# Output projection and MLP: squares in their own tiles, x of two residuals and the first MLP operands loaded ahead, sums of later quarters started earlier

## The chip, the cores and the metric

The kernel runs on one core of a Trainium2 chip. TensorE (PE) multiplies, VectorE (DVE) and ScalarE (ACT) do elementwise work, GpSimd (POOL) does little here, and SyncE (SP) issues nearly all transfers. The metric is the device time of one execution in microseconds (us).

## The reference

One layer of a hybrid decoder over 2048 tokens of width 1024, all in float32. Two token mixers fill `mix`; then come the output projection, the MLP and a gated embedding:

```python
mix_out = jnp.einsum('btc,cd->btd', mix, w_out[i])
h = h + rms_norm(mix_out, post_mix_norm[i])

u = jnp.einsum('btd,df->btf', rms_norm(h, pre_mlp_norm[i]), w_mlp_up[i])
y = jnp.einsum('btf,fd->btd', jnp.square(jax.nn.relu(u)), w_mlp_down[i])
h = h + rms_norm(y, post_mlp_norm[i])

e = rms_norm(jnp.einsum('bte,ed->btd', p[i], w_ple_proj[i]), ple_norm[i])
gate = jax.nn.sigmoid(jnp.einsum('btd,de->bte', h, w_ple_gate[i]))
h = h + e * gate
```

`rms_norm(x, w)` is x · rsqrt(mean(x²) + eps) · w over the width. The MLP is 4096 wide.

## The kernel before

Each float32 operand is split into a high part (a copy by ACT to fp32r, line 165 or 218) and a low part (a subtraction by DVE, line 166 or 219), and a product of 128x128 by 128x512 is three matmuls: high·high, high·low, low·high. Work is transposed: a tile holds 128 of the width and a quarter of 512 tokens.

**Output projection (about 1122 to 1307 us).** The loop over `order` takes quarter q = 0..3 and block d = 0..7; each pair is 24 matmuls `mmo`, and ACT copies the bank to `yo` (line 1361). For q = 0 and 1 ACT also squares the bank into `sq_o` and DVE adds it to `acc_o` (lines 228, 229). `sq` is one tile, shared by `sq_o`, `sq_h` and `rr`. At the end of quarters 0 and 1 `normed` starts: `rstd_steps` sums over the width by two matmuls with ones (`nrm_o`, lines 1152 and 1153, from `hl_o`, the split of `acc_o`), then makes the reciprocal root (Ln, Exp, one correction step); `residual` scales each of the eight blocks, adds x (loaded two at a time into `late` tiles, `xo`), stores h to `h1d`, and sums the squares in `acc_h`; a second `rstd_steps` (`nrm_h`) gives the scale for the MLP. For q = 2 and 3 `yo` goes to memory (`yod`) and its norm comes later.

`w_out` is split anew for quarters 0 to 2. For the last quarter, blocks below `RESTS` load the raw weights and the stored low part, and ACT makes the high part (line 349); the others are loaded split from a 1 MB cache (line 186).

**MLP up, half 0 (from about 1307 us).** Sixteen groups g, each seven Strassen products of 12 matmuls (`u`, 84 matmuls a group). The moving operands `t11 .. t22` come from `early_operands` (`be`, quarter 0) and `up_operands` (`b`, quarter 1), which load h from `h1d` and scale it; `run(prep)` finishes what is left of them before the MLP. The weights of the next group (`a`, `s`, split as `wu`) are prepared by `up_weights` between the products. DVE adds each product into `u` (line 1471) and forms `ht` (1452 to 1455). `summed(q)` squares quarters 2 and 3 from `yod` (`nrm_o2`, `nrm_o3`), and `passed(q)` makes their residual (`yp`, `xp`, `nrm_h2`, `nrm_h3`).

**What sets the order.** Every eight matmuls a tick runs an agenda. `later(gen, steps)` gives a generator's next step to the tick with that offset. PE's order is the order of the code with its ticks; in the output projection the orders of DVE, ACT and SP are set by a scheduler. On each engine the queue then runs in order, so an instruction that waits holds all behind it. Moving operands lie in 28 ring slots, `y` in 16 tiles, `stg` in two.

Of the kernel before, what the change touches and what calls it, by code (L numbers as in the profile page):

```python
# [10 lines left out]
F32 = mybir.dt.float32  # L11
# [4 lines left out]
ALU = mybir.AluOpType  # L16
# [68 lines left out]
def trunk(ctx, tc, x, xT, pT, vecs, w_in, w_ab, gdn_a_log, gdn_dt_bias, w_out, w_up, w_down,  # L85
# [38 lines left out]
    def col(r):  # L124
        return cols[:, r : r + 1]
# [95 lines left out]
    def squares(acc, src, k, name, eng=V):  # L221

        if acc is None:
            acc = st.tile([P, QT], F32, tag="acc", name=f"acc_{name}", bufs=3)
            S.activation(acc, src, AF.Square)
        else:
            sq = st.tile([P, QT], F32, tag="sq", name=f"sq_{name}_{k}", bufs=1)
            S.activation(sq, src, AF.Square)  # L228
            eng.tensor_tensor(acc, acc, sq, ALU.add)  # L229
        return acc  # L230
# [905 lines left out]
    def ytile(name):  # L1136
        return f2.tile([P, QT], F32, tag="y", name=name, bufs=16)
# [38 lines left out]

    kept_rows = []

    def residual(q, y_of, rsb, skip, gain, dst, name, sums=None):

        xk = late(skip(0), f"x{name}{q}_0")
        y = y_of(0)
        total, put = None, None
        for d in range(KD):
            yield
            if put:
                nc.sync.dma_start(*put)
            if d + 1 < KD:
                nxt, ynxt = late(skip(d + 1), f"x{name}{q}_{d + 1}"), y_of(d + 1)
            V.scalar_tensor_tensor(y, y, col(gain + d), rsb, ALU.mult, ALU.mult)  # L1190
            V.tensor_tensor(y, y, xk, ALU.add)
# [8 lines left out]
    def normed(q, ys, acc, skip, gain, dst, name, sums=None, pool=None):  # L1200

        rd = []
        yield from rstd_steps(acc, 1.0 / D, EPS, f"{name}{q}", rd.append, pool)
        total = yield from residual(q, lambda d: ys[d], rd[0], skip, gain, dst, name, sums)
# [38 lines left out]
    def moving(half, n, k, raw):  # L1243
        x = next_pool().tile([P, 2, QT], F32R, tag="ring", name=f"t{n}_{half}_{k}")
        split(x, V, raw)
        tops[half][n].append(x)

    def start_operands(half):
        tops[half] = {n: [] for n in ("11", "3", "1", "2", "21", "4", "22")}

    first_b = {}

    def early_operands():

        start_operands(0)
        for k in range(KD // 2):
            for n, kk in (("11", k), ("21", k + KD // 2)):
                b = first_b[kk] = ytile(f"be_{kk}")
                nc.sync.dma_start(b, h1d[0][kk])
                V.scalar_tensor_tensor(b, b, col(R_PREMLP + kk), h1_r[0], ALU.mult, ALU.mult)  # L1260
                moving(0, n, k, b)
                yield

    def up_operands(half, rsb):

        qs = (2 * half, 2 * half + 1)
        early = half in tops
        if not early:
            start_operands(half)
        for k in range(KD // 2):  # L1270
            n = f"{half}_{k}"
            b11, b21, b12, b22, t3, t2, t4 = (once(lambda i=i: ytile(f"b{i}_{n}")) for i in range(7))
            if early:
                b11, b21 = (lambda k=k: first_b[k]), (lambda k=k: first_b[k + KD // 2])
            for b, s, kk in ((b12, 1, k), (b22, 1, k + KD // 2), (b11, 0, k), (b21, 0, k + KD // 2)):
                if early and s == 0:
                    continue
                nc.sync.dma_start(b(), h1d[qs[s]][kk])
                V.scalar_tensor_tensor(b(), b(), col(R_PREMLP + kk), rsb[s], ALU.mult, ALU.mult)
# [45 lines left out]
    for j, (q, d) in enumerate(order):  # L1325
        if d == 0:
            ys, acc = [], None
            if q < 2:
                later(mix_operands(q + 1), range(2, 18, 2))
            if q == 1:  # L1330
                later(mix_operands(3), range(17, 25))
        ready_out(j + 2)
        stage_out(j + 3)
        if j == len(order) - 5:
            u_raw = [wp.tile([P, 2, QT], F32, tag="raw", name=f"u_raw{i}", bufs=2) for i in range(2)]
            a1, a2 = w_up[0], w_up[FF // P // 2]
            for t, i, src in ((u_raw[0], 0, a1[:, : KD // 2]), (u_raw[1], 1, a1[:, KD // 2 :]),
                              (u_raw[0], 1, a2[:, : KD // 2]), (u_raw[1], 0, a2[:, KD // 2 :])):
                nc.sync.dma_start(t[:, i].rearrange("p (k n) -> p k n", n=P), src)
        if j == len(order) - 2:  # L1340
            two_blocks(("11", u_raw[0][:, 0]), ("12", u_raw[1][:, 1]))
        if j == len(order) - 1:
            (a11, a21), (s1, s4) = ((t[:, 0], t[:, 1]) for t in u_raw)
            b22 = two_blocks(("22", s1), None)
            V.tensor_tensor(s1, s1, a21, ALU.add)
# [24 lines left out]
    V.tensor_tensor(a11, s1, a11, ALU.subtract)  # L1370
    u_block("2", b2, a11)
# [419 lines left out]
```

## Time and profile before

| | us |
|---|---|
| median of the runs | 2741.42 (2741.19 to 2742.86) |
| profiled execution | 2737.24 |
| its span | 2735.0 |
| PE busy | 2663.3 (97%) |
| DVE busy | 2046.1 (75%) |
| ACT busy | 1471.4 (54%) |

Times of the trace count from the span's start. A row of the timeline has start, duration, engine, line, operation, tiles, count, and in brackets the idle time before it with what released it; numbers in tile names are left out there. A row of a table of windows has, after the window and its length, the busy time and count of PE, PEld, DVE, ACT and POOL, the granted PE clock as a share of full speed, the DMA engines' busy share and GB/s; where only PE is shown the other engines are missing.

### The profile page before, as it was taken

To read this page: it belongs to the slowest core of one execution; us is meant where nothing else is said; L and a number is where in the kernel's file an instruction comes from. 1 tells how busy PE (TensorE), PEld (TensorE's weight loads), DVE (VectorE), ACT (ScalarE), POOL (GpSimd) and SP (SyncE) were. 2 spreads that over 40 slices of the span, in tenths; PEclk is the share of its full clock that TensorE was granted. 3 is DMA by queue.
4 is the path that set the end of the run, shared out by engine and by line. 5 is a ranking of instruction groups with operands and counts; after the bars stand their busy time and mean duration, and the time that the engine had idled before them with its cause. 6 is when DMAs were issued, how large, how long until landed. Compare 5 with 4: busy or idle time off the path is not lost. (4 is left out here: it accounts for less than half of the span.)

```text
span 2735.0 us, 38459 instructions
## 1 busy us (share of the span) xinstructions
PE 2663.3 (97%) x12745; PEld 2216.0 (81%) x12745; DVE 2046.1 (75%) x4245; ACT 1471.4 (54%) x2949; POOL 105.2 (4%) x104
## 2 busy tenths in 40 slices
PE   6999999999999999999999999999999999999999
PEld 5788788888888888778787888887888888887887
DVE  6788877787788777677788977857787765568775
ACT  6666555455546445675466656545455545465431
POOL 0000000000000000000000000001000000001000
PEclk9999999999999999999999999999999999999999
DMA  7777777666666665878456757667454346577663
GB/s 265 248 244 238 230 250 244 220 223 238 239 206 216 214 213 169 268 270 285 137 184 225 250 186 237 223 194 245 151 203 159 141 173 205 194 255 247 208 220 123
DMA packets 271766, 590.81 MB, mean 216 GB/s; under 512 B 55994, under 2 KB 60568, under 8 KB 253648
## 3 DMA queue, kind: packets, MB, share of 16 engines
q1 hardware_dynamic: 271568, 588.36, 63.5%
q8 instruction: 101, 1.65, 0.2%
q14 instruction: 97, 0.79, 0.1%
HBM read 423.94 MB, written 164.30 MB: 215 GB/s over the span
## 5 line engine op out<-in xcount | busy, mean ns | idle before, releaser
L1052 PE MATMUL mm<-xt,w 128*128 128x512 f32 x3072 | 783.4, 401 | 2.8 <-ACT qk_h L787 1.5
L1052 PEld LDWEIGHTS mm<-xt,w 128*128 128x128 f32 x3072 | 556.9, 189 | 107.8 <-ACT qk_h L787 2.0
L1121 PE MATMUL d<-db,da 128*128 128x512 f32 x2688 | 613.1, 390 | 4.7 <-DVE db L219 3.3
L1121 PEld LDWEIGHTS d<-db,da 128*128 128x128 f32 x2688 | 504.1, 188 | 112.9 <-DVE db L219 6.4
L1121 PE MATMUL u<-t,wu 128*128 128x512 f32 x2604 | 593.7, 390 | 0.9 <-ACT wu L165 0.8
L1121 PEld LDWEIGHTS u<-t,wu 128*128 128x128 f32 x2604 | 490.5, 188 | 103.3 <-ACT wu L165 1.2
L219 DVE TENSOR_TENSOR db<-db 128x512 fp32r<-128x512 f32 x224 | 160.9, 718 | 73.3 <-ACT db L218 72.3
L1471 DVE TENSOR_TENSOR u<-u,u 128x512 f32<-128x512 f32 x224 | 150.8, 684 | 61.1 <-PE u L1121 60.1
L218 ACT ACTIVATE db<-db 128x512 fp32r<-128x512 f32 x224 | 140.7, 628 | 83.1 <-DMA db<-hid 81.7
L1121 PE MATMUL mmg<-h2T,wg 128*128 128x512 f32 (+1 forms) x792 | 174.7, 383 | 0.0
L1121 PE MATMUL mmo<-mixT,w_out 128*128 128x512 f32 x720 | 166.1, 392 | 3.3 <-ACT sq_o L228 2.2
L1121 PEld LDWEIGHTS mmg<-h2T,wg 128*128 128x128 f32 x792 | 145.7, 188 | 28.9
L1512 ACT ACTIVATE u<-u 128x512 f32<-128x512 f32 x128 | 80.8, 631 | 161.6 <-DVE u L1471 160.9
L1121 PEld LDWEIGHTS mmo<-mixT,w_out 128*128 128x128 f32 x720 | 136.2, 189 | 32.3 <-ACT sq_o L228 2.6
L166 DVE TENSOR_TENSOR da<-da 128x512 fp32r<-128x512 f32 x128 | 94.4, 737 | 86.8 <-ACT da L165 86.4
L165 ACT ACTIVATE da<-da 128x512 fp32r<-128x512 f32 x128 | 80.4, 628 | 135.0 <-DMA da<-sumd 112.6
L165 ACT ACTIVATE wu<-a 128x512 fp32r<-128x512 f32 x124 | 74.2, 623 | 56.6 <-DMA a<-in_w_up_dram 55.0
L687 DVE TENSOR_TENSOR pr_g<-xs_g,sys_g 128x16 f32<-128x16 f32 (+14 forms) x240 | 93.9, 391 | 5.3
L229 POOL TENSOR_TENSOR acc_y<-acc_y,sq_y 128x512 f32<-128x512 f32 x28 | 38.7, 1381 | 1377.6 <-ACT sq_y L228 1377.6
L166 DVE TENSOR_TENSOR wu<-a,wu 128x512 fp32r<-128x512 f32 x124 | 85.1, 689 | 8.1 <-ACT wu L165 8.1
L1513 ACT ACTIVATE u<-u 128x512 f32<-128x512 f32 x128 | 80.7, 630 | 3.5
L166 DVE TENSOR_TENSOR da<-dr,da 128x512 fp32r<-128x512 f32 x96 | 66.4, 692 | 18.9 <-ACT da L165 16.9
(381 smaller groups left out, 3808.6 us busy)
## 6 DMA issues: line engine op xcount, KB each, us to landing
w<-cache_in SPq DMA_DIRECT2D x96, 1024.0 KB
db<-hid SPq DMA_DIRECT2D x224, 256.0 KB
cache_in<-w SPq DMA_DIRECT2D x32, 1024.0 KB
hid<-u SPq DMA_DIRECT2D x128, 256.0 KB
da<-sumd SPq DMA_DIRECT2D x128, 256.0 KB
a<-in_w_up_dram SPq DMA_DIRECT2D x124, 256.0 KB
hid<-ht SPq DMA_DIRECT2D x96, 256.0 KB
dr<-in_w_down_dram SPq DMA_DIRECT2D x96, 256.0 KB
```

The lines of the kernel that those rows point to most:

```text
L165: S.activation(t[:, 0], raw, AF.Copy)
L166: eng.tensor_tensor(t[:, 1], raw, t[:, 0], ALU.subtract)
L218: S.activation(t[:, 0], plain(t), AF.Copy)
L219: V.tensor_tensor(t[:, 1], plain(t), t[:, 0], ALU.subtract)
L229: eng.tensor_tensor(acc, acc, sq, ALU.add)
L687: V.tensor_tensor(pr[:, :, :, 0:i], xs[:, None, :, 0:i].broadcast_to([P, 2, GC, i]), sys[:, 0:i, i : i + 2].rearrange("p j two -> p two j" ...
L1052: PE.matmul(ps, *terms[i], start=i == 0, stop=i == nt - 1)
L1121: PE.matmul(ps, a, b, start=start, stop=stop)
L1471: V.tensor_tensor(c[new], c[old], ps, ALU.add)
L1512: S.activation(c[k], c[k], AF.Relu)
L1513: S.activation(c[k], c[k], AF.Square)
```

## The change

- The output's squares `sq_o` of quarters 0 and 1 get tiles of their own, the two `stg` tiles.
- The last step of `normed(1)`, which holds `nrm_h1`, goes from tick 25 to tick 21; what depends on it, `prep`, begins one block earlier.
- `RESTS` goes from 5 to 6, so block 5 of the last quarter is built from raw weights and the stored low part.
- `skip_ahead` loads x for the residuals of quarters 0 and 1 during the quarter itself, two blocks in a transfer, into ring tiles `xa`. `mix_operands(3)` gets ticks 27 to 34 in place of 17 to 24.
- `early_operands` and `up_operands` load one step ahead of the scaling.
- `summed(2)` and `summed(3)` start at g = 1 and 3, before at 2 and 6, and `passed(2)` and `passed(3)` still at 5 and 9, with other steps.

```diff
-OUT_STEPS = (1, 5) + tuple(range(7, 15)) + (15, 25)
+OUT_STEPS = ((1, 5) + tuple(range(7, 15)) + (15, 25), (1, 5) + tuple(range(7, 15)) + (15, 21))
...
-            sq = st.tile([P, QT], F32, tag="sq", name=f"sq_{name}_{k}", bufs=1)
+            sq = scratch() if scratch else st.tile([P, QT], F32, tag="sq", name=f"sq_{name}_{k}", bufs=1)
...
-    staged_out, ready, rests, RAW, RESTS = {}, {}, {}, 3, 5
+    staged_out, ready, rests, RAW, RESTS = {}, {}, {}, 3, 6
...
+    def skip_ahead(q):
+
+        for d in range(0, KD, 2):
+            t = next_pool().tile([P, 2, QT], F32, tag="ring", name=f"xa{q}_{d}")
+            nc.sync.dma_start(t, xT[d * P : (d + 2) * P, tok(q)].rearrange("(k p) t -> p k t", p=P))
+            x_ahead.extend((t[:, 0], t[:, 1]))
+            yield
...
         for k in range(KD // 2):
-            n = f"{half}_{k}"
-            b11, b21, b12, b22, t3, t2, t4 = (once(lambda i=i: ytile(f"b{i}_{n}")) for i in range(7))
             if early:
-                b11, b21 = (lambda k=k: first_b[k]), (lambda k=k: first_b[k + KD // 2])
+                for kk in ((0, 1) if k == 0 else (k + 1,)):
+                    if kk < KD // 2:
+                        fetch(kk)
+            else:
+                fetch(k)
+            b11, b21, b12, b22, t3, t2, t4 = got.pop(k)
...
             if q < 2:
                 later(mix_operands(q + 1), range(2, 18, 2))
+                later(skip_ahead(q), (20, 22, 24, 26))
             if q == 1:
-                later(mix_operands(3), range(17, 25))
+                later(mix_operands(3), range(27, 35))
...
-            acc = squares(acc, ps, d, f"o{q}")
+            acc = squares(acc, ps, d, f"o{q}",
+                          scratch=lambda: tp.tile([P, QT], F32, tag="stg", name=f"sqo{q}_{d}"))
...
-            later(normed(q, ys, acc, lambda d, q=q: xT[blk(d), tok(q)], R_POSTMIX, h1d[q], "o", "h"), OUT_STEPS)
+            later(normed(q, ys, acc, lambda d, q=q: xT[blk(d), tok(q)], R_POSTMIX, h1d[q], "o", "h",
+                         late=ready_x), OUT_STEPS[q])
...
-            if half == 0 and g in (2, 6):
-                later(summed((g + 2) // 4 + 1), list(range(2, 20, 2)) + [20, 24, 28])
+            if half == 0 and g in (1, 3):
+                later(summed((g + 3) // 2), list(range(2, 20, 2)) + [20, 30, 33])
             if half == 0 and g in (5, 9):
-                later(passed((g + 3) // 4), list(range(2, 38, 4)) + [40, 46, 50])
+                later(passed((g + 3) // 4), list(range(2, 29, 3)) + [29, 36, 39])
```

First place: PE's queue around `nrm_h1`, the sum over the width of quarter 1's h. In `mmo_2_7` the numbers are quarter and block. Before:

```order
L1121 MATMUL mmo_2_7_13405<-mixT2_6_12872,w_out23_13294 128x512 x3
L1121 MATMUL mmo_2_7_13405<-mixT2_7_12907,w_out23_13294 128x512 x3
L1121 MATMUL mmo_3_0_13444<-mixT3_0_12919,w_out24_13349 128x512 x3
L1121 MATMUL mmo_3_0_13444<-mixT3_1_12942,w_out24_13349 128x512 x3
L1121 MATMUL mmo_3_0_13444<-mixT3_2_12954,w_out24_13349 128x512 x2
L1152 MATMUL nrm_h1_13453<-hl_h1_13301,ones_70 128x512
L1153 MATMUL nrm_h1_13453<-hl_h1_13301,ones_70 128x512
```

With the change:

```order
L1121 MATMUL mmo_2_6_13340<-mixT2_5_12832,w_out22_13221 128x512 x3
L1121 MATMUL mmo_2_6_13340<-mixT2_6_12864,w_out22_13221 128x512 x3
L1121 MATMUL mmo_2_6_13340<-mixT2_7_12899,w_out22_13221 128x512 x3
L1152 MATMUL nrm_h1_13392<-hl_h1_13287,ones_70 128x512
L1153 MATMUL nrm_h1_13392<-hl_h1_13287,ones_70 128x512
L1121 MATMUL mmo_2_7_13391<-mixT2_0_12637,w_out23_13280 128x512 x3
L1121 MATMUL mmo_2_7_13391<-mixT2_1_12669,w_out23_13280 128x512 x3
```

`nrm_h1` moved from the first block of quarter 3 to between blocks 6 and 7 of quarter 2, 32 matmuls earlier. At the same place DVE's queue, from the last block's x (`xo`, or `xa` with the change) to the split `hl_h1` that `nrm_h1` reads. Before:

```order
L1191 TENSOR_TENSOR yo1_7_13025<-yo1_7_13025,xo1_7_13256 128x512
L166 TENSOR_TENSOR t11_0_2_13358<-be_2_13355,t11_0_2_13358 128x512
L1260 SCALAR_TENSOR_TENSOR be_6_13369<-be_6_13369,cols_92,rn0_13051 128x512
L229 TENSOR_TENSOR acc_h1_13147<-acc_h1_13147,sq_h1_7_13274 128x512
L1260 SCALAR_TENSOR_TENSOR be_3_13383<-be_3_13383,cols_92,rn0_13051 128x512
L166 TENSOR_TENSOR t21_0_2_13372<-be_6_13369,t21_0_2_13372 128x512
L166 TENSOR_TENSOR hl_h1_13301<-acc_h1_13147,hl_h1_13301 128x512
L166 TENSOR_TENSOR t11_0_3_13386<-be_3_13383,t11_0_3_13386 128x512
L1260 SCALAR_TENSOR_TENSOR be_7_13406<-be_7_13406,cols_92,rn0_13051 128x512
L166 TENSOR_TENSOR t21_0_3_13409<-be_7_13406,t21_0_3_13409 128x512
L1156 TENSOR_SCALAR acc_h1_13147<-nrm_h1_13453 128x512
```

With the change:

```order
L1191 TENSOR_TENSOR yo1_7_12993<-yo1_7_12993,xa1_6_13037 128x512
L166 TENSOR_TENSOR w_out23_13280<-raw_out23_13224,w_out23_13280 128x1024
L229 TENSOR_TENSOR acc_h1_13131<-acc_h1_13131,sq_h1_6_13244 128x512
L166 TENSOR_TENSOR t21_0_0_13293<-be_4_13263,t21_0_0_13293 128x512
L166 TENSOR_TENSOR t11_0_1_13307<-be_1_13290,t11_0_1_13307 128x512
L229 TENSOR_TENSOR acc_h1_13131<-acc_h1_13131,sq_h1_7_13258 128x512
L166 TENSOR_TENSOR t21_0_1_13321<-be_5_13304,t21_0_1_13321 128x512
L166 TENSOR_TENSOR t11_0_2_13344<-be_2_13318,t11_0_2_13344 128x512
L166 TENSOR_TENSOR hl_h1_13287<-acc_h1_13131,hl_h1_13287 128x512
L1279 SCALAR_TENSOR_TENSOR be_6_13341<-be_6_13341,cols_92,rn0_13017 128x512
L1279 SCALAR_TENSOR_TENSOR be_3_13355<-be_3_13355,cols_92,rn0_13017 128x512
L1156 TENSOR_SCALAR acc_h1_13131<-nrm_h1_13392 128x512
```

From `acc_o1<-nrm_o1`, which lies further ahead, to `hl_h1` the queue had 44 rows and has 41. Two `be` scalings and two splits now stand behind `hl_h1`, and a split of `w_out` stands after the last addition of x.

Second place: PE's queue around `nrm_o3`, the sum over the width of quarter 3's output, in the MLP. In `u4_0_5` the numbers are the product, the half and the group. Before:

```order
L1121 MATMUL u12_0_8_15378<-t21_0_1_13335,wu12_0_8_15191 128x512 x3
L1121 MATMUL u12_0_8_15378<-t21_0_2_13372,wu12_0_8_15191 128x512 x3
L1121 MATMUL u12_0_8_15378<-t21_0_3_13409,wu12_0_8_15191 128x512 x3
L1152 MATMUL nrm_o3_15415<-hl_o3_15326,ones_70 128x512
L1153 MATMUL nrm_o3_15415<-hl_o3_15326,ones_70 128x512
L1121 MATMUL u2_0_8_15408<-t2_0_0_13538,wu2_0_8_15223 128x512 x3
L1121 MATMUL u2_0_8_15408<-t2_0_1_13618,wu2_0_8_15223 128x512 x3
```

With the change:

```order
L1121 MATMUL u4_0_5_14925<-t22_0_0_13511,wu4_0_5_14725 128x512 x3
L1121 MATMUL u4_0_5_14925<-t22_0_1_13601,wu4_0_5_14725 128x512
L1152 MATMUL nrm_o3_14930<-hl_o3_14739,ones_70 128x512
L1153 MATMUL nrm_o3_14930<-hl_o3_14739,ones_70 128x512
L1121 MATMUL u4_0_5_14925<-t22_0_1_13601,wu4_0_5_14725 128x512 x2
L1121 MATMUL u4_0_5_14925<-t22_0_2_13675,wu4_0_5_14725 128x512 x3
L1121 MATMUL u4_0_5_14925<-t22_0_3_13754,wu4_0_5_14725 128x512 x3
```

It moved from between the second and third product of group 8 into the last product of group 5. DVE's queue around the row that reads it. Before:

```order
L166 TENSOR_TENSOR hl_o3_15326<-acc_o3_15003,hl_o3_15326 128x512
L229 TENSOR_TENSOR acc_h2_14842<-acc_h2_14842,sq_h2_6_15323 128x512
L1452 TENSOR_TENSOR ht1_0_7_15342<-u_0_7_15151,u11_0_7_15187 128x512
L1190 SCALAR_TENSOR_TENSOR yp2_7_15319<-yp2_7_15319,cols_92,rsb_po2_14767 128x512
L1453 TENSOR_TENSOR u_0_7_15151<-u22_0_7_15256,u_0_7_15151 128x512
L1454 TENSOR_TENSOR ht2_0_7_15343<-u22_0_7_15256,ht1_0_7_15342 128x512
L1191 TENSOR_TENSOR yp2_7_15319<-yp2_7_15319,xp2_7_15317 128x512
L1455 TENSOR_TENSOR ht4_0_7_15344<-u21_0_7_15274,ht2_0_7_15343 128x512
L1156 TENSOR_SCALAR acc_o3_15003<-nrm_o3_15415 128x512
L229 TENSOR_TENSOR acc_h2_14842<-acc_h2_14842,sq_h2_7_15412 128x512
```

With the change:

```order
L1490 TENSOR_TENSOR ht4_0_4_14753<-u21_0_4_14693,ht2_0_4_14752 128x512
L166 TENSOR_TENSOR wu11_0_6_14781<-a11_0_6_14758,wu11_0_6_14781 128x512
L1448 TENSOR_TENSOR s1_0_6_14784<-a21_0_6_14760,a22_0_6_14762 128x512
L1156 TENSOR_SCALAR acc_o3_14449<-nrm_o3_14930 128x512
L1449 TENSOR_TENSOR a21_0_6_14760<-a11_0_6_14758,a21_0_6_14760 128x512
L1506 TENSOR_TENSOR u11_0_5_14806<-u_0_5_14779,u12_0_5_14787 128x512
L166 TENSOR_TENSOR wu12_0_6_14810<-a12_0_6_14764,wu12_0_6_14810 128x512
L1453 TENSOR_TENSOR s2_0_6_14813<-s1_0_6_14784,a11_0_6_14758 128x512
L1506 TENSOR_TENSOR u_0_5_14779<-u_0_5_14779,u2_0_5_14823 128x512
L1190 SCALAR_TENSOR_TENSOR yp2_0_14800<-yp2_0_14800,cols_92,rsb_po2_14796 128x512
```

The row `acc_o3<-nrm_o3` stood behind the `ht` rows of group 7; now it stands behind the first weight rows for group 6 and ahead of the first addition of group 5 (`u11_0_5`). Behind `nrm_o3`, PE has 216 matmuls to `nrm_h2`, and DVE has 82 rows from this row to `hl_h2`.

More of the change, by code (lines that the diff above doesn't have):

```diff
@@ L219, in split_in_place, with squares @@
         V.tensor_tensor(t[:, 1], plain(t), t[:, 0], ALU.subtract)
-    def squares(acc, src, k, name, eng=V):
+    def squares(acc, src, k, name, eng=V, scratch=None):
         if acc is None:
@@ L1177, in trunk, with residual @@
     kept_rows = []
-    def residual(q, y_of, rsb, skip, gain, dst, name, sums=None):
+    def residual(q, y_of, rsb, skip, gain, dst, name, sums=None, late=late):
         xk = late(skip(0), f"x{name}{q}_0")
@@ L1198, in residual, with normed @@
         return total
-    def normed(q, ys, acc, skip, gain, dst, name, sums=None, pool=None):
+    def normed(q, ys, acc, skip, gain, dst, name, sums=None, pool=None, late=late):
         rd = []
         yield from rstd_steps(acc, 1.0 / D, EPS, f"{name}{q}", rd.append, pool)
-        total = yield from residual(q, lambda d: ys[d], rd[0], skip, gain, dst, name, sums)
+        total = yield from residual(q, lambda d: ys[d], rd[0], skip, gain, dst, name, sums, late)
         if sums is not None:
@@ L1249, in start_operands, with ready_x @@
         tops[half] = {n: [] for n in ("11", "3", "1", "2", "21", "4", "22")}
+    x_ahead = []
+    def skip_ahead(q):
[4 more added lines that the diff above has]
+            yield
+    def ready_x(src, name):
+        return x_ahead.pop(0)
     first_b = {}
@@ L1255, in early_operands, with fetch @@
         start_operands(0)
[L1256 to L1262, printed above, removed]
+        each = [(n, k, kk) for k in range(KD // 2) for n, kk in (("11", k), ("21", k + KD // 2))]
+        def fetch(kk):
+            first_b[kk] = ytile(f"be_{kk}")
+            nc.sync.dma_start(first_b[kk], h1d[0][kk])
+        fetch(each[0][2])
+        for i, (n, k, kk) in enumerate(each):
+            if i + 1 < len(each):
+                fetch(each[i + 1][2])
+            V.scalar_tensor_tensor(first_b[kk], first_b[kk], col(R_PREMLP + kk), h1_r[0], ALU.mult, ALU.mult)
+            moving(0, n, k, first_b[kk])
+            yield
     def up_operands(half, rsb):
@@ L1269, in up_operands, with fetch @@
             start_operands(half)
+        got = {}
+        def fetch(k):
+            n = f"{half}_{k}"
+            b = [once(lambda i=i: ytile(f"b{i}_{n}")) for i in range(7)]
+            if early:
+                b[0], b[1] = (lambda: first_b[k]), (lambda: first_b[k + KD // 2])
+            for i, s, kk in ((2, 1, k), (3, 1, k + KD // 2), (0, 0, k), (1, 0, k + KD // 2)):
+                if not early or s:
+                    nc.sync.dma_start(b[i](), h1d[qs[s]][kk])
+            got[k] = b
         for k in range(KD // 2):
-            n = f"{half}_{k}"
-            b11, b21, b12, b22, t3, t2, t4 = (once(lambda i=i: ytile(f"b{i}_{n}")) for i in range(7))
             if early:
-                b11, b21 = (lambda k=k: first_b[k]), (lambda k=k: first_b[k + KD // 2])
+                for kk in ((0, 1) if k == 0 else (k + 1,)):
[4 more added lines that the diff above has]
+            b11, b21, b12, b22, t3, t2, t4 = got.pop(k)
             for b, s, kk in ((b12, 1, k), (b22, 1, k + KD // 2), (b11, 0, k), (b21, 0, k + KD // 2)):
[L1276 to L1279, printed above, removed]
+                if not early or s:
+                    V.scalar_tensor_tensor(b(), b(), col(R_PREMLP + kk), rsb[s], ALU.mult, ALU.mult)
             yield
```

## The prediction

> **What bounds the kernel now.** The page's busy times come first, then the list of PE's waits, then a table of time windows, then the timeline around each wait.
>
> ```profile
> PE 2663.3 (97%) x12745; PEld 2216.0 (81%) x12745; DVE 2046.1 (75%) x4245; ACT 1471.4 (54%) x2949; POOL 105.2 (4%) x104
> ...
> PE nrm_o L1152 <- ACT hl_o L165: 6.0, 1, 6.0
> ...
> PE u L1121 <- ACT w_u L165: 3.6, 1, 3.6
> ...
> PE mmo L1121 <- ACT sq_o L228: 2.2, 1, 2.2
> ```
>
> PE is busy 97% of the span, so only PE's own idle time can be won, and the change adds no matmul. PE's waits in the part that is edited are the three above (sum, count, longest) and one of 1.05 us for a transfer. What each costs is read from windows: PE busy, matmul count, then the granted clock (third figure from the end).
>
> ```profile
> 1200.00:1220.00 20.00, 17.80 (x73) 14.29 (x71) 19.38 (x29) 11.61 (x18) 0.00 (x0) 0.91 0.81 277
> 1280.00:1310.00 30.00, 28.95 (x128) 23.67 (x127) 24.23 (x39) 16.89 (x30) 0.00 (x0) 1.00 0.76 275
> 1310.00:1330.00 20.00, 16.38 (x65) 12.74 (x64) 11.40 (x19) 4.24 (x7) 0.00 (x0) 0.91 0.07 27
> 1450.00:1500.00 50.00, 43.31 (x179) 35.01 (x178) 41.98 (x69) 29.27 (x49) 0.00 (x0) 0.93 0.64 214
> 2000.00:2100.00 100.00, 100.00 (x443) 82.87 (x442) 79.78 (x128) 55.46 (x93) 0.00 (x0) 1.00 0.47 167
> ...
> 1215.60:1219.00 3.40, 3.31 (x8) 0.52 0.89 278
> 1317.00:1321.00 4.00, 4.00 (x12) 0.61 0.19 70
> 1478.00:1482.00 4.00, 2.26 (x5) 0.53 0.97 308
> 1290.90:1294.00 3.10, 3.10 (x14) 1.00 1.06 435
> ```
>
> The undisturbed window gives 100/443 = 0.2257 us a matmul. At that pace the first four windows should take 16.5, 28.9, 14.7 and 40.4 us, so they lose 3.5, 1.1, 5.3 and 9.6 us. The first, third and fourth lose 1.3, 1.7 and 2.9 us more than their waits (2.2, 3.6, and 6.0 + 0.7): after each the clock stands at 0.52 to 0.61 for some microseconds. After the wait of 1.05 us it stays 1.00. So a wait of 2 us or more costs itself and 1.3 to 1.7 us; the longest counts twice, as it delays two matmuls.
>
> On this row a rule can be weighed. The Trainium skill, "TensorE: Matmul & The Clock Gate", section "HAM oscillation", sums its rule up as no idle gaps of PE over about 3.4 us. Here a gap of 2.2 us was already followed by clock 0.52, so the measurement goes ahead of it. By the rule the new short waits below would cost only themselves, and the sum would be about 4 us lower, by estimate.
>
> **Quarter 1's squares.**
>
> ```profile
> 1204.03 0.63 ACT L228 ACTIVATE sq_h<-yo 128x512 f32<-128x512 f32 x1 [1.72 <-DVE acc_h L229]
> ...
> 1215.04 0.60 ACT L228 ACTIVATE sq_o<-mmo 128x512 f32<-128x512 f32 x1 [1.05 <-DVE acc_h L229]
> ...
> 1215.69 3.56 PE L1121 MATMUL mmo<-mixT,w_out 128*128 128x512 f32 x8 [2.20 <-ACT sq_o L228]
> ```
>
> sq_o and sq_h share one tile, so ACT waits for DVE's adds, which wait for that residual's chain; sq_o reads PE's bank, and PE waits for the bank. With tiles of their own the output's squares no longer wait for acc_h. I take the whole loss: −3.5 us (bounds −3.5 and −2.4, the latter if half of the 2.2 us stays because DVE's add of sq_o, which frees the new tiles in turn, still stands behind the residual's rows).
>
> **Quarter 1's residual and the earlier nrm_h1.** Step 21 in place of 25 puts nrm_h1 32 matmuls earlier: 128 behind nrm_o1, before 160.
>
> ```profile
> 1227.02 0.39 PE L1153 MATMUL nrm_o<-hl_o,ones 128*128 128x512 f32 x1
> ...
> 1229.84 0.69 DVE L1156 TENSOR_SCALAR acc_o<-nrm_o 128x512 f32<-128x512 f32 x1
> ...
> 1253.07 0.69 DVE L1191 TENSOR_TENSOR yo<-yo,xo 128x512 f32<-128x512 f32 x1 [1.43 <-DMA xo<-in_xT_dram]
> ...
> 1257.05 0.69 DVE L1191 TENSOR_TENSOR yo<-yo,xo 128x512 f32<-128x512 f32 x1 [0.95 <-DMA xo<-in_xT_dram]
> ...
> 1263.20 0.69 DVE L166 TENSOR_TENSOR hl_h<-acc_h,hl_h 128x512 fp32r<-128x512 f32 x1
> ...
> 1263.94 0.19 PEld L1153 LDWEIGHTS nrm_h<-hl_h,ones 128*128 128x128 f32 x1 [0.46 <-DVE hl_h L166]
> ```
>
> DVE's stretch from acc_o to the end of hl_h takes 34.05 us. x loaded ahead takes away the two xo waits (2.4 us), and the order has 41 rows where 44 stood, 3 × 0.68 = 2.0 us. That leaves 29.6. It starts 2.6 us after the matmul slot behind nrm_o (1227.02 + 0.22, to 1229.84), so hl_h ends 32.2 after that slot. PE arrives after 128 × 0.2257 + 0.2 = 29.1. The matmul is 3.1 late, loses 1.3 of clock, and gives up the 0.46 of before: +3.9 us. Bounds: DVE at 0.62 us a row, the pace of five rows below in 3.09 us, needs 41 × 0.62 = 25.4 and is early, −0.5; with the xo waits replaced by others it is 5.5 late, +6.7. Behind the late nrm_h1 all of PE waits; DVE's b rows, which need it, have 40 us until the MLP.
>
> The four double loads for x carry the bytes of the eight single ones. They take ring slots, and mix_operands(3) is scheduled ten ticks later for it; the splits of mixT3 stay near quarter 1's end in DVE's order, over 35 us (1227 to 1264 is still quarter 2) ahead of their use: nothing. On SP an `xa` load may wait for its slot, and the raw `w_out` loads queue behind it; those are issued three blocks ahead, 72 × 0.2257 = 16 us, which covers one late slot. If two slots came late in a row PE would wait for w_out, 2 to 5 us; nothing in the rows shows such a wait on SP, so it stays out of the sum.
>
> **Sixth rest.** PE's 1.05 us below waits for a 1 MB reload. It becomes 512 KB and a copy of 1.05 us on ACT, which is 54% busy: −1.1 us (bounds 0 and −1.1). The store in quarter 0 halves.
>
> **Start of the MLP.**
>
> ```profile
> 1290.89 16.64 PE L1121 MATMUL mmo<-mixT,w_out 128*128 128x512 f32 x72 [1.05 <-DMA w_out<-cache_out]
> ...
> 1296.98 0.92 SPq L1278 DMA_DIRECT2D b<-h1d  x2
> ...
> 1301.93 0.75 DVE L1279 SCALAR_TENSOR_TENSOR b<-b,cols,rn 128x512 f32<-128x512 f32 x1 [4.07 <-DMA b<-h1d]
> ...
> 1307.97 3.09 DVE L166 TENSOR_TENSOR t<-b,t 128x512 fp32r<-128x512 f32 x5
> ...
> 1310.98 0.69 DVE L1345 TENSOR_TENSOR u_raw<-u_raw,u_raw 128x512 f32<-128x512 f32 x1
> ...
> 1315.91 0.63 ACT L165 ACTIVATE w_u<-u_raw 128x512 fp32r<-128x512 f32 x1 [1.90 <-DVE u_raw L1370]
> 1316.60 15.79 PE L1121 MATMUL u<-t,w_u 128*128 128x512 f32 x60 [3.62 <-ACT w_u L165]
> ```
>
> The last b pair is issued at 1296.98 and DVE stands 4.07 us for it; from 1301.93 on DVE has a row almost without a gap until w_u at 1316. Fetched one k earlier the pair is there, and DVE gains 4.07 where PE waits 3.62: −5.3 us with its clock. Bounds: −5.3, and 0 if the t tiles still get their ring slots only when PE's last block of quarter 3 has read mixT3, which both versions need.
>
> **Sums of quarters 2 and 3 in the MLP.**
>
> ```profile
> 1396.50 0.39 PE L1153 MATMUL nrm_o<-hl_o,ones 128*128 128x512 f32 x1
> ...
> 1396.93 0.69 DVE L1156 TENSOR_SCALAR acc_o<-nrm_o 128x512 f32<-128x512 f32 x1 [2.58 <-PE nrm_o L1153]
> ...
> 1479.05 0.80 PE L1152 MATMUL nrm_o<-hl_o,ones 128*128 128x512 f32 x1 [6.00 <-ACT hl_o L165]
> ...
> 1479.80 0.68 DVE L166 TENSOR_TENSOR hl_o<-acc_o,hl_o 128x512 fp32r<-128x512 f32 x1
> ...
> 1480.54 0.80 PE L1153 MATMUL nrm_o<-hl_o,ones 128*128 128x512 f32 x1 [0.70 <-DVE hl_o L166]
> ...
> 1505.85 0.68 DVE L1156 TENSOR_SCALAR acc_h<-nrm_h 128x512 f32<-128x512 f32 x1
> ...
> 1567.58 0.69 DVE L166 TENSOR_TENSOR hl_h<-acc_h,hl_h 128x512 fp32r<-128x512 f32 x1
> ```
>
> Before, nrm_o3 waits 6.0 + 0.7 us since DVE has two tasks at once, summed(3) and passed(2): 117 rows from acc_o2 to hl_o3 in 82.87 us, 0.708 us a row. With the sums starting one and three groups earlier, summed(3) is over before passed(2) begins, and that wait goes: −9.6. But the new order puts acc_o3 on DVE ahead of all of group 5's u adds, while PE reaches nrm_o3 only 76 matmuls into that group of 84. DVE stands there for a good part of it (a group is 84 × 0.2257 = 19.0 us), and seven weight splits for group 6 and the u adds queue behind. From there it is 82 rows to hl_h2, and PE has 216 matmuls, 48.8 us, to nrm_h2. With passed alone DVE made 95 rows (acc_h2 to hl_h3) in 61.73 us, 0.650 a row. So hl_h2 comes 0.4 + 82 × 0.650 + 0.5 = 54.2 after nrm_o3, 5.4 late. The pieces fall on the weights of groups 7 and 8 or on nrm_h2; two to four of them cost 2.9 us of clock: +8.3. Then acc_h2 to hl_h3: 110 × 0.650 = 71.5 against 336 × 0.2257 = 75.8: no wait. Net −1.3. Bounds: at 0.62 a row 2.8 late and 1.3 of clock, net −5.5; at 0.708, 10.2 late and then 3.0 at hl_h3, 4.6 of clock, net +8.2. I stay with 0.650, since its rows are of the same mix.
>
> **Sum.** −3.5 + 3.9 − 1.1 − 5.3 − 1.3 = −7.3 us. The profiled execution took 2737.24 us; −7.3 makes 2729.9. The median of the runs stands 4.2 above that execution, at 2741.42, and moves alike: 2734.1.
>
> **Rivals.** (1) No new wait: DVE runs at 0.62 or the scheduler's rows bear waiting. All four losses and the 0.46 go, 20.0 us: 2721.4. For it: DVE is only 75% busy. Against it: both new waits follow from counted rows. (2) The MLP's first wait stays, by the ring slots: −2.0, 2739.4. For it: t rows still stand between the last b and w_u. Against: DVE's 4.07 us row is a transfer. (3) Slower: DVE, held at nrm_o3, never catches up. Lateness at hl_h2 and hl_h3 together is 192p − 122.8 us for p us a row; with 4.6 of clock it passes the 5.5 us of slower from p = 0.73. At 0.735 the time is about 2748. For it: 0.708 was already seen with two tasks. Against: one task now.
>
> **How the numbers follow.** 0.2% is 5.5 us, about what can be told from no change. Chances: the forecast 0.50 (own range 2729 to 2739, two thirds of it below 2735.9), rival 1 0.20, rival 2 0.22, rival 3 0.08. Faster: 0.33 + 0.20 + 0.04 (of rival 2, where one new wait is missing too) = 0.57; slower 0.08; the same 0.35. The range 2720 to 2744 runs from rival 1 to the bound of 0.708 a row (2743.6).
>
> **What the next profile would show.** In the list of PE's waits mmo on sq_o, w_out on the cache, u on w_u and nrm_o on hl_o are gone; a wait of about 3 us of nrm_h on hl_h stands near 1257; DVE waits 5 us or more for nrm_o in group 5 (near 1430), and waits of u on wu and of nrm_h on hl_h follow by 1490, each with a dip of the clock. Without the first I am wrong on nrm_h1; without the second on DVE's order; with w_u still waiting on the MLP's start.

## The result and the profile after

| kernel | median, us (runs) | ratio to before (95%) | profiled execution, us | its span, us |
|---|---|---|---|---|
| before | 2742.56 (16) | 1 | 2737.24 | 2735.0 |
| with the change | 2736.89 (16) | 0.9977 (0.997 to 0.9985) | 2733.76 | 2731.9 |

The change makes the kernel 0.23% faster: 5.7 us by the medians, 6.3 by the ratio. The forecast was -7.3. In a later set of runs the same kernel stood at 0.9961 (0.9949 to 0.9973), so each estimate lies outside the other's interval, and differences of a few microseconds between sets can't be told from none. Stretches of single profiles are therefore used to say where time went, and several profiles where there are some. The profile of before, at 2737.24 us, lies at the low end of that kernel's times: the 16 runs in the table go from 2737.01 to 2748.83.

The list of PE's waits between the first `mmo` of the output projection and the first `d` of the MLP's down half, kernel with the change (engine, line, tile, releaser: sum, count, longest, in us):

```profile
PE u L1121 <- ACT wu L165: 3.2, 2, 2.4
PE mmo L1121 <- DVE w_out L166: 2.5, 1, 2.5
PE u L1121 <- DVE wu L166: 1.1, 2, 0.9
PE u L1121 <- ACT u L1531: 0.8, 1, 0.8
...
PE nrm_h L1153 <- DVE hl_h L166: 0.6, 1, 0.6
```

The waits shown of before (6.0, 3.6, 2.2 us and the 1.05 for the cache) are gone, and a new set stands in their place. What that comes to, by PE's own landmarks (start of the first row of each group in PE's timeline, us between them; each column one profile):

| stretch of PE | before | change | change, second profile | forecast |
|---|---|---|---|---|
| first `mmo` to `nrm_o1` | 103.85 | 104.26 | 101.82 | -3.5 |
| `nrm_o1` to first `u` of the MLP | 80.57 | 80.17 | 80.69 | +3.9 - 1.1 |
| first `u` to first product of group 1 | 25.85 | 20.06 | 20.06 | -5.3 |
| from there to first `d` | 297.60 | 295.72 | 294.54 | -1.3 |
| sum | 507.87 | 500.21 | 497.11 | -7.3 |

So the sum came out near the forecast, -7.7 and -10.8 against -7.3 (the whole spans fell by 3.1 and 7.3). The output projection gained 0 to 1.9 us, the start of the MLP 5.8, the rest of MLP up 1.9 to 3.1. The parts of the program that the change does not touch moved too, from one profile to the next: ahead of the first `mmo` 1122.95, 1125.29 and 1126.55 us, behind the first `d` 1104.2, 1106.4 and 1104.0 us. The column of before is one profile: the kernel of the first experiment below, whose rows on DVE in quarter 1 stand in the same order as before, took 106.49 us for the first stretch.

PE's timeline of the start of the MLP with the change, to be held against the row at 1316.60 of before:

```profile
1309.72 19.23 PE L1121 MATMUL u<-t,w_u 128*128 128x512 f32 x84
1329.78 55.98 PE L1121 MATMUL u<-t,wu 128*128 128x512 f32 x244 [0.83 <-ACT wu L165]
```

All 84 matmuls of group 0 run without a gap; only the 0.8 us before group 1 stays, as it was.

The two places at which a new wait was forecast, in the timelines of DVE and PE with the change:

```profile
1424.78 0.69 DVE L1156 TENSOR_SCALAR acc_o<-nrm_o 128x512 f32<-128x512 f32 x1 [8.32 <-PE nrm_o L1153]
...
1477.80 0.68 DVE L166 TENSOR_TENSOR hl_h<-acc_h,hl_h 128x512 fp32r<-128x512 f32 x1
...
1446.43 19.36 PE L1121 MATMUL u<-t,wu 128*128 128x512 f32 x84 [0.83 <-ACT u L1531]
1468.13 11.22 PE L1121 MATMUL u<-t,wu 128*128 128x512 f32 x40 [2.35 <-ACT wu L165]
1479.19 0.39 PE L1152 MATMUL nrm_h<-hl_h,ones 128*128 128x512 f32 x1
...
1260.38 0.50 PE L1153 MATMUL nrm_h<-hl_h,ones 128*128 128x512 f32 x1 [0.65 <-DVE hl_h L166]
```

DVE stands 8.32 us at `acc_o3` in group 5. From there it takes 53.02 us to `hl_h2`, 82 rows at 0.647 us. PE pays in two pieces, at group 7 (0.83) and group 8 (2.35), and reaches `nrm_h2` with no wait left there. `nrm_h1` waits only 0.65 us.

The wait that nobody put into the sum is the one on `w_out`:

```profile
1202.81 1.21 DVE L166 TENSOR_TENSOR w_out<-raw_out,w_out 128x1024 fp32r<-128x1024 f32 x1
...
1212.06 1.22 DVE L166 TENSOR_TENSOR w_out<-raw_out,w_out 128x1024 fp32r<-128x1024 f32 x1
...
1213.33 3.91 PE L1121 MATMUL mmo<-mixT,w_out 128*128 128x512 f32 x9 [2.49 <-DVE w_out L166]
```

Two splits of `w_out` stand 9.25 us apart on DVE, and PE's blocks are 24 × 0.2257 = 5.4 us. Between them is quarter 0's residual. The second split has no idle time of DVE just ahead of it, here and in every other profile in which `mmo` waits for `w_out`; in the second profile DVE had worked off 36 rows without a gap of 0.1 us. So what PE waits for there is the place of the split in DVE's queue, and not the transfer of the raw weights.

### The profile page after: what moved, and what is told of

Its sections match the earlier page's. It is cut to its first block, busy times and chain, and to the rows that moved or that the text cites. A ratio compares the mean times of both kernels' runs of the same rounds, so it can differ in the third digit from the quotient of the medians.

```text
span 2731.9 us, 38444 instructions
## 1 busy us (share of the span) xinstructions
PE 2664.7 (98%) x12745; PEld 2214.7 (81%) x12745; DVE 2043.4 (75%) x4245; ACT 1472.0 (54%) x2950; POOL 105.3 (4%) x104
## 5 line engine op out<-in xcount | busy, mean ns | idle before, releaser
L1121 PEld LDWEIGHTS mmg<-h2T,wg 128*128 128x128 f32 x792 | 145.5, 188 | 29.1
L229 POOL TENSOR_TENSOR acc_y<-acc_y,sq_y 128x512 f32<-128x512 f32 x28 | 38.6, 1379 | 1371.7 <-ACT sq_y L228 1371.7
L692 DVE SCALAR_TENSOR_TENSOR xs_g<-xs_g,sys_g 128x4 f32<-128x4 f32 x256 | 57.6, 225 | 29.1 <-DMA sys_g<-ud_g 24.0
```

The costliest lines, as they stand in the source:

```text
L692: V.scalar_tensor_tensor(xs[:, :, i + 1], xs[:, :, i], sys[:, i, i + 1 : i + 2], xs[:, :, i + 1], ALU.mult, ALU.add)
L1121: PE.matmul(ps, a, b, start=start, stop=stop)
```

## Experiments

First the kernels that undo or isolate one part of the change, then those that try to mend it. Ratios are to the kernel before, which was run again with each set.

### The first MLP operands loaded ahead, alone

```diff
+# before.py with early_operands and up_operands of the change
```

> Kernel before with one part of the change alone: the first MLP operands are loaded one step ahead. Theory (the load of the last b pair holds DVE 4.07 us and with it the MLP's first weights): the 3.6 us wait of u on w_u goes, PE's stretch from the first u to the first product of group 1 falls from 25.85 to about 20.1 us, and the time by 5 to 6 us. Rival (the ring slots, which the t tiles get only from the last block of quarter 3, set the start): the stretch stays over 24 us and the time within 1 us. Rival (the gain needs the earlier nrm_h1): half of it stays, stretch 22 to 24.

Ratio 0.9992 (0.9983 to 1.0001). PE's timeline:

```profile
1315.94 19.69 PE L1121 MATMUL u<-t,w_u 128*128 128x512 f32 x84
1336.46 3.83 PE L1121 MATMUL u<-t,wu 128*128 128x512 f32 x14 [0.83 <-ACT wu L165]
```

The start of the MLP takes 20.52 us, and 25.85 before: this part alone is worth the 5.3 us there, without the earlier `nrm_h1`, and the ring slots do not hold it. The time shows less, 2.2 us by the ratio where 5 to 6 were forecast. In this profile the wait on `sq_o` had 4.5 us where the one of before had 2.2, and first `mmo` to `nrm_o1` took 106.49 us, though DVE's order there is the same row for row: that wait is not of a fixed size. Whether it hides the rest of the gain is not shown, as this profile is the slowest of the kernel's 11 runs.

### The output's squares back in one tile

```diff
-                          scratch=lambda: tp.tile([P, QT], F32, tag="stg", name=f"sqo{q}_{d}"))
+                          scratch=None)
```

> Changed kernel, with the output's squares back in the one shared tile. Theory (DVE sets the end of quarter 1): the wait on sq_o comes back and the one on w_out shrinks or goes; the stretch of PE from the first mmo to nrm_o1 stays within 1 us of 104.3, and the time within 1 us of the changed kernel's. Rival (the prediction's own term: the tiles are worth 3.5 us): stretch 107 to 108, time 3 to 4 us more.

Ratio 0.9986 (0.9977 to 0.9995). PE's timeline:

```profile
1212.18 7.10 PE L1121 MATMUL mmo<-mixT,w_out 128*128 128x512 f32 x30 [1.51 <-DVE w_out L166]
...
1260.03 0.50 PE L1152 MATMUL nrm_h<-hl_h,ones 128*128 128x512 f32 x1 [2.52 <-ACT hl_h L165]
```

Neither forecast is quite right. First `mmo` to `nrm_o1` takes 102.13 us, within the 101.2 to 104.3 of six profiles with tiles of their own and the change's order there; no wait on `sq_o` came back, so in the changed kernel the tiles do not gain their 3.5 us where the prediction put them. But `nrm_h1` now waits 2.52 + 0.70 us, and `nrm_o1` to the first `u` takes 84.94. First `mmo` to first `u` is then 187.07 us, and 182.5 to 184.4 in four profiles with two tiles and step 21: the tiles are worth 2.6 to 4.6 us after all, one stretch later. The scheduler's order on DVE changed with the tile, so not all of it need be the tile itself.

### Quarter 1's adds on POOL

```diff
-            acc = squares(acc, ps, d, f"o{q}",
+            acc = squares(acc, ps, d, f"o{q}", eng=G if q == 1 else V,
```

> Changed kernel, with quarter 1's adds of the output's squares (7 of acc_o) on POOL in place of DVE. Theory (DVE sets the end of quarter 1: it is 98% busy from 1190 to 1216 us in both kernels, so freeing the square tile only moved PE's wait from sq_o to w_out): DVE loses 7 x 0.69 = 4.8 us of work, the 2.5 us wait of mmo on w_out goes, and PE's stretch from the first mmo to nrm_o1 falls from 104.3 us to 100.5 to 101.5; the time falls by about 3 us against the changed kernel. Rival (the raw weights land late, ACT waited 0.75 us for them): the w_out wait stays at 2 us or more and the stretch at 103.5 to 104.5. Rival (POOL's adds, 1.38 us each elsewhere in the program, hand the two tiles back too late): a wait on sqo of 1 us or more in its place.

Ratio 1.0 (0.999 to 1.0009). Windows of 1190 to 1213 us, this kernel first and the changed one second; then DVE's scaling rows (line 1190) from 1190 to 1215 in the same order (busy, mean ns):

```profile
1190.00:1213.00 23.00, 19.92 (x89) 16.18 (x88) 23.00 (x31) 14.71 (x25) 7.71 (x4) 1.00 0.80 275
```

```profile
1190.00:1213.00 23.00, 20.84 (x92) 16.90 (x91) 22.46 (x34) 18.41 (x32) 0.00 (x0) 1.00 0.86 293
```

```profile
L1190 DVE SCALAR_TENSOR_TENSOR yo<-yo,cols,r_o 128x512 f32<-128x512 f32 x8 | 8.8, 1130 | 0.0
```

```profile
L1190 DVE SCALAR_TENSOR_TENSOR yo<-yo,cols,r_o 128x512 f32<-128x512 f32 x8 | 5.8, 742 | 0.0
```

DVE had fewer rows and was just as busy: three of the eight scalings, each begun while an add of POOL ran, take 1.77 to 1.79 us and raise the mean from 742 to 1130 ns. POOL's own six adds from 1190 on take 2872 ns on average, and 1379 elsewhere. The wait on `w_out` was 3.1 us, that of `nrm_h1` 4.0, and first `mmo` to first `u` took 191.12. So this kernel does not relieve DVE, and does not test the theory.

### x loaded late again

```diff
-                later(skip_ahead(q), (20, 22, 24, 26))
...
-                         late=ready_x), OUT_STEPS[q])
+            later(normed(...), OUT_STEPS[q])
```

> Changed kernel without skip_ahead: the residuals load x block by block as before. Theory: DVE's stretch from acc_o1 to the end of hl_h1, 29.1 us in every kernel with x ahead, rises to 31 to 33 by waits on xo, and nrm_h1 waits as much longer: 2 to 4 us, first mmo to first u 186 to 188, time +2 to +5. Rival (x ahead is worth nothing, since its loads only move): stretch 29 to 30, the waits as in the changed kernel.

Ratio 1.0018 (1.0008 to 1.0027), the slowest of all. The list of PE's waits from 1195 to 1300 us:

```profile
PE nrm_h L1152 <- ACT hl_h L165: 9.2, 1, 9.2
PE mmo L1121 <- DVE w_out L166: 2.7, 2, 2.2
```

DVE's stretch from `acc_o1` to the end of `hl_h1` took 35.39 us where every other kernel at step 21 with two tiles and `mix_operands(2)` unmoved has 29.1. First `mmo` to first `u` is 195.37 us, and 182.5 to 184.4 in the two profiles of the change. The forecast sign is right and its size too small. Of the 6.3 us that the stretch grew, DVE's waits for `xo` are 1.3; three more rows are 2.1, and waits for ACT the rest (a split of `w_out` alone waits 2.30). So in this profile x loaded ahead acts through the order more than through its own transfers, and without it the earlier `nrm_h1` waits 9.2 us.

### RESTS back at 5

```diff
-    staged_out, ready, rests, RAW, RESTS = {}, {}, {}, 3, 6
+    staged_out, ready, rests, RAW, RESTS = {}, {}, {}, 3, 5
```

> Changed kernel with RESTS back at 5, so block 5 of the last quarter is loaded split, 1 MB, from the cache. Theory: PE's wait on w_out from the cache near 1290 comes back with 1.0 us and nothing else moves by more than a microsecond. Rival (the DMA engines' load then is lower in the changed kernel, x being loaded before): no wait, no change.

It was made from the kernel of tick 24 below, and not from the changed one. Ratio 0.9953 (0.994 to 0.9965), against 0.9944 (0.9931 to 0.9958) of its base in another set. There was no wait on the cache. The list of PE's waits from 1195 to 1330 us shows others:

```profile
PE mmo L1121 <- DVE w_out L166: 3.8, 1, 3.8
PE nrm_h L1152 <- ACT hl_h L165: 1.7, 1, 1.7
PE nrm_h L1153 <- DVE hl_h L166: 0.6, 1, 0.6
```

So the 1.05 us that the forecast gave to the sixth rest is gone without it too; which part of the change took them is not shown. But first `mmo` to first `u` is 189.18 us, and 182.84 in its base, more than the profiles of one order differ among themselves (182.5 to 184.4). DVE's order in quarter 1 is another with five rests, and `w_out` waits 1.3 us longer than in any of those. So the sixth rest may be worth some microseconds in another place than forecast; one profile doesn't settle it, and the ratios of the two sets overlap.

### The sums of quarters 2 and 3 at their old places

```diff
+            if half == 0 and g in (2, 6):
+                later(summed((g + 2) // 4 + 1), list(range(2, 20, 2)) + [20, 24, 28])
             if half == 0 and g in (5, 9):
+                later(passed((g + 3) // 4), list(range(2, 38, 4)) + [40, 46, 50])
```

> Changed kernel, with summed and passed at the groups and steps of before. Theory (the earlier sums trade the 9.6 us stall at nrm_o3 for about 6 us behind DVE's hold in group 5 and 1.3 us in group 12): the 6 us wait of nrm_o3 on hl_o3 comes back, the waits of u on wu in groups 6 to 13 go, and PE's stretch from the first product of group 1 to the first d rises from 295.7 to about 297.6; time +2 us. Rival (the early sums are worth their whole 9.6): +8 to +10. Rival (worth nothing): within 0.5 of 295.7.

Ratio 0.9972 (0.9961 to 0.9984), the same as with the change. The list of PE's waits behind group 0:

```profile
PE nrm_o L1152 <- ACT hl_o L165: 5.2, 1, 5.2
PE u L1121 <- ACT wu L165: 0.8, 1, 0.8
PE nrm_o L1153 <- DVE hl_o L166: 0.7, 1, 0.7
```

The stretch takes 296.82 us against 295.72 and 294.54: the earlier sums as they were made are worth 1.1 to 2.3 us of the 9.6 lost at `nrm_o3`.

### `nrm_o3` at tick 24

```diff
-                later(summed((g + 3) // 2), list(range(2, 20, 2)) + [20, 30, 33])
+                later(summed((g + 3) // 2), list(range(2, 20, 2)) + [20, 24, 27])
```

> Changed kernel, with the steps of summed [20, 24, 27] in place of [20, 30, 33], so PE comes to nrm_o3 48 matmuls earlier, when DVE reaches the row that reads it. Theory (PE's waits in groups 6 to 8 come from DVE standing 8.3 us at acc_o3): DVE's wait there falls under 2 us, the waits of u of 0.83 and 2.35 us and the slow clock behind them go, nrm_o3 to nrm_h2 is at PE's pace, and the time falls by 4 to 6 us. Rival (DVE's total work in groups 5 to 8 sets it): the waits stay, at most -1 us. Rival (hl_o3 is not ready so early): a new wait of 1 us or more of nrm_o on hl_o, which takes back half or more.

Ratio 0.9944 (0.9931 to 0.9958), median 2724.70. DVE's and PE's timelines:

```profile
1412.21 0.69 DVE L1156 TENSOR_SCALAR acc_o<-nrm_o 128x512 f32<-128x512 f32 x1 [2.21 <-PE nrm_o L1153]
...
1411.78 0.39 PE L1153 MATMUL nrm_o<-hl_o,ones 128*128 128x512 f32 x1
1412.01 60.00 PE L1121 MATMUL u<-t,wu 128*128 128x512 f32 x264
1471.85 0.39 PE L1152 MATMUL nrm_h<-hl_h,ones 128*128 128x512 f32 x1
```

DVE's wait falls from 8.32 to 2.21 us, and all of PE's waits in MLP up but the 0.8 us at group 1 are gone, those of group 12 too. The stretch falls to 287.93 us, 6.6 to 7.8 less than with the change. That is what the hold cost, and it is the largest single item found. (The same steps move `nrm_o2`; there DVE waits 3.49 us in place of none, and PE nowhere.)

### With it, `nrm_h1` back at step 25

```diff
+OUT_STEPS = (..., (1, 5) + tuple(range(7, 15)) + (15, 25))
```

> Kernel of tick 24, with nrm_h1 back at step 25. Theory (nrm_h1 32 matmuls earlier costs the little that PE waits for hl_h1, 0.8 + 0.7 us, and the start of the MLP doesn't need it): those two waits go and the stretch from nrm_o1 to the first u falls by 1 to 2 us to 79 to 80; the start of the MLP stays at 20.1. Time -1 to -2 us against tick 24. Rival (the earlier nrm_h1 is what gives the last b loads their lead): a wait of u on w_u or of DVE on b of 2 us or more comes back, time +2 to +5.

Ratio 0.9936 (0.9923 to 0.995). The list of PE's waits from 1195 to 1330 us:

```profile
PE mmo L1121 <- DVE w_out L166: 2.5, 1, 2.5
PE u L1121 <- ACT wu L165: 0.8, 1, 0.8
```

The waits on `hl_h1` go, `nrm_o1` to the first `u` takes 78.88 us in place of 80.93, and the MLP starts as before (20.19). In the sum, first `mmo` to first `u`, it is 183.17 against 182.84, since `w_out` cost more in this profile, and the times can't be told apart.

### With it, quarter 2's operands earlier

```diff
-                later(mix_operands(q + 1), range(2, 18, 2))
+                later(mix_operands(q + 1), range(2, 18, 2) if q == 0 else range(0, 8))
```

> Kernel of tick 24, with the loads and splits of quarter 2's operands in the first eight ticks of quarter 1 in place of every second of sixteen, so 3 DVE rows (2 us) less stand between r_o0 and the split of the w_out block that PE waits for near 1213, and 1180 to 1190, where DVE is 50% busy, takes them. Theory (DVE's rows in that stretch set the wait): the wait of mmo on w_out (0.9 to 2.5 us in kernels with the same order there) goes; first mmo to nrm_o1 100 to 101 us. Rival (the raw weights' transfers set it; the DMA engines are 90% busy and more there): the wait stays at 1 to 3 us, the stretch at 101 to 104.

Ratio 0.9959 (0.9947 to 0.9971), against 0.9944 of its base in another set; the intervals overlap, but first `mmo` to first `u` is 190.32 us where the base has 182.84. `w_out` still waits, 2.1 us in two pieces; the first stretch takes 102.54. And `nrm_h1` waits 5.3 us: `acc_o1` starts 4.8 us after `nrm_o1` on DVE (1.4 to 2.3 in kernels with the change's order there), and its stretch takes 31.2. Neither of the two splits waited for its transfer: DVE had no idle time just ahead of them. Taking three rows away ahead of one split moved the lateness down the queue.

### Residual spread, with tick 24 and step 25

```diff
-OUT_STEPS = ((1, 5) + tuple(range(7, 15)) + (15, 25), ...
+OUT_STEPS = ((1, 5, 7, 8, 10, 11, 13, 14, 16, 17, 18, 26), ...
```

> Kernel of tick 24 with step 25, and quarter 0's residual spread over three more ticks, so that the split of the w_out block that PE waits for near 1213 stands 6 rows (about 4 us) further ahead on DVE. Theory (DVE's rows ahead of that split set the wait): the wait on w_out of 2.5 us falls under 0.7, the first mmo to nrm_o1 takes 100 to 101.5 us, and nrm_o1 to the first u stays at 79 to 80, since nrm_h1 has 32 matmuls of slack; time -2 to -3 us against the same kernel without it. Rival (DVE's whole budget of quarter 1 must be paid somewhere): another wait in the output projection takes it back, first mmo to first u 182.5 to 184.5 as in the others. Rival (the raw weights' transfers): the wait on w_out stays.

> The kernel of tick 24 with step 25 once more, to stand beside the spread one. Expected: first mmo to first d 490.5 to 491.5; w_out's wait 0.9 to 2.5; no wait of nrm_h on hl_h.

The spread kernel has 2722.23 us, ratio 0.9929 (0.9916 to 0.9942); its twin without the spread 2725.36, ratio 0.994 (0.9928 to 0.9952). The spread one waits on `w_out` 1.3 and 0.4 us, the twin 2.3. But first `mmo` to first `u` is 181.04 against 181.45: the difference is too small to be told, and `acc_o1` starts 5.3 us after `nrm_o1`, where the twin has 2.1. The 32 matmuls of slack at step 25 keep that from PE. So the gain of 2 to 3 us is not shown; the rival's 182.5 to 184.5 was missed too, by spread and twin alike. The twin's first `mmo` to first `d`, forecast at 490.5 to 491.5, was 489.55. The spread kernel has the lowest ratio, 0.3 to 0.5% below that of the change, and most of that is the hold.

### The change once more

> The changed kernel once more, for the spread of its waits from one profile to the next. Expected: 500 us +- 1.5 from the first mmo to the first d; the waits in the MLP (0.83, 2.35, 0.93, 0.8 us) the same within 0.3, since DVE's queue sets them, and the wait on w_out near 1213 anywhere from 0.9 to 2.5 us, as in kernels with the same order there.

Ratio 0.9961, median 2729.53. First `mmo` to first `d` took 497.11 us, outside the forecast of 500 +- 1.5. In MLP up the waits of u on wu repeat (3.4 us by ACT's rows and 1.3 by DVE's, where the first profile had 3.2 and 1.1), the one of 0.8 us for a bank is missing. `w_out` waits 1.6 us, and `nrm_h1` 0.6 + 0.6.

## Why the prediction was right, and where it was not

**The sum: right, and in part by luck.** The start of the MLP and the hold at `nrm_o3` came as forecast. In the output projection, held against the profile of before, -3.5 was 1.5 to 3.9 us off and +3.9 about 3 us off the other way. The prediction did not know that the two hang together; that they nearly cancelled was luck.

**Start of the MLP: right.** -5.3 forecast, -5.8 measured, and 5.3 from this part alone. The rival of the ring slots is ruled out by that experiment.

**The hold at `nrm_o3`: right in mechanism and in size.** Forecast were a DVE wait of 5 us or more (8.32), 0.650 us a row (0.647), a net of -1.3 (-1.9 and -3.1), and +8.3 for the hold. Taking the hold away gave 6.6 to 7.8. The forecast put the lateness on `nrm_h2` or the weights; it fell on the weights and on one bank. It also said that `hl_h3` costs nothing; `nrm_h3` waited 0.12 us, and the weights of group 12 0.93.

**Quarter 1's squares: the place wrong, the size not settled.** The term was -3.5. Against the profile of before the first stretch moved by +0.4 and -2.0, and against the other profile with the same order (106.49) by -2.2 and -4.7. The step that failed took the whole loss as the tile's and put nothing in its place. The wait on `sq_o` did go, but a wait on `w_out` of 0.9 to 2.5 us came in every profile with the change's order there. In the very row that was quoted for the loss, 1200 to 1220, DVE was busy 19.38 of 20 us, and from 1190 to 1213 it was busy 22.46 of 23 with the change. The next thing late there was another product of DVE's queue, the split of `w_out`. The text named `w_out` as a possible wait, for ring slots on SP, and kept it out of the sum; the cause it should have priced was DVE.

**`nrm_h1`: DVE's stretch right, its start wrong.** 29.6 us were forecast for the stretch, 29.1 measured in each of nine profiles with x ahead, two tiles and `mix_operands(2)` unmoved. But it starts 1.4 to 2.3 us after `nrm_o1` with the change's order, not 2.8. Of +3.9 about +1 came (without the sixth rest's 1.05 us the second stretch moved by +0.7 and +1.2). By the prediction's own sign, a wait of about 3 us near 1257, it was wrong here: 0.65 and 0.61 + 0.64 came. These two errors are one: at both places PE waits for the same queue, and most of what it waits at the first it saves at the second. Four profiles have step 21 and the same order on DVE: the change twice, the old sums, tick 24. There the wait on `w_out` was 2.49, 1.64, 0.93 and 1.72 us, the start 1.4, 2.0, 2.3 and 2.2 us behind `nrm_o1`, and the wait of `nrm_h1` 0.70, 1.25, 1.59 and 1.45, so both waits together 2.5 to 3.2. With the start 3.1 us late (one shared tile) it waits 2.52 + 0.70, and with 4.8 (operands earlier) 5.3. That DVE's whole load sets the sum of both is what all these kernels agree with; no run took load off DVE in that stretch cleanly, so it is argued and not shown.

**Sixth rest: not borne out.** The 1.05 us went, but it went without this part too. What the part is worth elsewhere stays open.

**The clock: right in kind, the limit not.** The prediction had every wait of 2 us or more cost 1.3 to 1.7 us of clock. Whether a wait costs clock is seen in the windows behind PE's waits of 2.49, 2.35, 0.83 and 0.65 us in the changed kernel, then of 1.33 us in the spread one and 1.51 in the one with a shared tile (PE busy, count, granted clock):

```profile
1213.33:1217.30 3.97, 3.97 (x10) 0.57 0.73 245
1468.10:1472.10 4.00, 3.96 (x11) 0.68 0.82 313
1446.43:1449.50 3.07, 3.07 (x13) 1.00 1.06 405
1260.40:1263.40 3.00, 3.00 (x13) 1.00 1.01 413
```

```profile
1217.90:1220.90 3.00, 3.00 (x13) 1.00 0.91 309
```

```profile
1212.18:1215.20 3.02, 3.02 (x13) 1.00 0.65 222
```

These six look like a limit between 1.5 and 2.2 us, but further rows show none. The kernel with tick 24 and step 25 was profiled twice. Behind a wait on `w_out` of 2.49 us its clock was halved, in the first row from 1.5 us after the wait's end; behind one of 2.35 us it was not. Their first stretches differ by 1.7 us, of which the waits themselves make 0.1. The third row is the change again, behind a wait of 1.79 us in the down half of the MLP:

```profile
1215.24:1218.65 3.41, 3.41 (x10) 0.50 0.86 282
```

```profile
1217.58:1221.00 3.42, 3.42 (x15) 1.00 0.65 220
```

```profile
1875.51:1879.20 3.69, 3.58 (x8) 0.54 0.85 298
```

Over all fourteen profiles, from 1139 us on, single waits of 1.69 to 2.55 us were followed by half the clock in some cases and not in others (1.69 and 1.79 were, 2.50 and 2.55 were not); all longer ones were, and shorter single ones were not. Two short waits in a row can do it too: behind 0.95 + 0.64 us at `nrm_h1` in the kernel with the old sums the clock was 0.55. So a wait of about 2 us costs clock in one profile and not in the next; what decides it is not shown. It is a good part of the spread of the first stretch. The Trainium skill, "TensorE: Matmul & The Clock Gate", section "HAM oscillation", sums its rule up as no idle gaps of PE over about 3.4 us; the traces differ, with half the clock behind 1.79 us, and the measurement decides. Of the forecast 1.3 us of clock at `nrm_h1` nothing came in the two profiles of the change.

## What to carry to other kernels

When an engine is busy almost without a gap in the windows around a stall (here DVE, 19.38 of 20 us), removing the wait that is named there may only move it: ask which of the engine's later rows is late next, and add up all the stretches that hang on its queue before a part is called worthless. Where an order is set by a scheduler, count the rows between an instruction and its reader on both engines: 82 rows at 0.650 us against 216 matmuls gave the hold's cost within 2 us, and 48 matmuls earlier for a small reduction was worth more than the whole of the earlier sums. Price a wait of PE of about 2 us with the clock behind it as a chance, not as a sum, and look at more than one profile before a wait of 1 to 3 us is given a cause.

## What the runs showed of the hardware

POOL's adds and some of DVE's rows slow each other. In the experiment with quarter 1's adds on POOL, three 128x512 scalings with two operands and a column on DVE took 1.77 to 1.79 us, each begun while an add of POOL ran; the five others took 0.74. Behind 1217 us two splits took 1.78 and 1.79 us in place of 0.68, and one of `w_out` 2.26 in place of 1.21. DVE's plain additions (678 and 681 ns) did not change, nor did the splits within a long add of POOL; that add took 7.5 us, the six from 1190 on 2872 ns on average, and such adds take 1379 elsewhere. Free time on POOL was thus no free time for DVE's work. The Trainium skill, "SBUF — State Buffer", section "SBUF: two separate sides", has the two take turns on a shared pair of ports, each for a whole instruction; the longer rows on both engines agree, though the additions, with two inputs as well, show no wait here.
